# A two-block network on one core: a list scheduler that keeps GpSimd and VectorE apart, with new TensorE durations and a new precedence table

## The chip, the cores and the metric

The kernel runs on one core of a Trainium2 chip (trn2). The core has TensorE (PE, with its weight loads as PEld), VectorE (DVE), ScalarE (ACT), GpSimd (POOL) and SyncE (SP), which issues every DMA here. The metric is the device time of one execution in microseconds (us), lower is better.

## The reference, cut to what matters

Input x is [256, 1024] in float32: 256 tokens. Two blocks follow each other.

```python
# first block
mod = silu(c) @ ada_w + ada_b                  # 6 vectors of 1024: a 1024 x 6144 matrix
u = modulate(rmsnorm(x), sh_mix, sc_mix)
p = u @ w_in                                   # 1024 x 2816
y_conv = conformer_conv(p[..., :1024])         # 31 causal taps on 512 channels, layer norm, silu
y_rwkv = rwkv7_mix(p[..., 1024:])              # 8 heads of 64, a recurrence over the 256 tokens
x = x + gt_mix * (concat(y_conv, y_rwkv) @ w_out)
u = modulate(rmsnorm(x), sh_ffn, sc_ffn)
x = x + gt_ffn * peer_ffn(u)                   # 8 heads, top 16 of 128 x 128 experts; 16384 rows of peer_u, peer_v
x = rmsnorm(x) * final_g
# second block
mod = silu(c_2) @ w_mod_2 + b_mod_2
h = modulate(rms_norm(x)); proj = h @ w_in_2
o_a = dsa_attention(...)                       # keys chosen by an indexer, 4 heads
o_b = moba_attention(...)                      # 4 heads
x = x + gt_m * ((sigmoid(gate_a) * (o_a @ w_br_dsa_2) + sigmoid(gate_b) * (o_b @ w_br_moba_2)) @ w_out_2)
x = x + gt_f * ((silu(g) * u_) @ w_down_2)     # g, u_ = split(modulate(rms_norm(x)) @ w_gate_up_2)
```

## The kernel before

**Arithmetic.** Every float32 weight tile of [128, 1024] is used as a sum of two parts: `wload` (line 1270) issues a DMA of 512 KB into `W_wraw`, a cast into `W_whi`, and a subtraction `W_wlo = W_wraw - W_whi`. Each product is then three products: high by high, high by low, low by high. `W_wraw`, `W_whi` and `W_wlo` have three buffers each, and they are shared by all weight tiles of the program. The experts are not gathered: the hidden values of all 16384 experts are computed (`hidden`, 128 tiles of `peer_u`), multiplied with a grid of gates that is zero but for the chosen experts (`gates`: one-hot tiles `OH_oij` and `OH_oj`, products of them in float16, results into `gH`), and multiplied with all of `peer_v` (`values`, 128 tiles).

**Stages**, in us from the start, where instructions of each first appear on VectorE or PE: modulation and first norm to 58; projections, convolution and RWKV in four chunks (`Mixer`) to 271; output projection, second norm, queries, scores and top 16 of both token tiles (`Peer.scores`, `topk`), with the first hidden columns beside them, to 479; hidden columns and gates to 828; `values` with the second block's modulation beside it to 1175; the final norm to 1196; the second block's projections, attention and second norm to 1455; and the rest of its feed-forward to the end.

**What sets the order.** The program is written as a straight line against recorders. `Recorder.record` (line 81) takes each call down with its dependencies, and `Schedule` (line 282) places them by list scheduling: at each moment each free engine takes the ready instruction with the largest bottom level (the longest chain of costs that hangs on it). [...] `PRIORITY` (line 761) moves the rank of groups of instructions by fixed amounts. Calls through `nc.any` may go to one of two engines: `tensor_tensor`, `tensor_scalar` and `memset` to DVE or POOL, `copy` to ACT or DVE; the engine that is free takes it unless `elsewhere` finds that the other would be done sooner. So `W_wlo`, `OH_oj`, the products into `gH` and others may run on POOL, while calls of `nc.gpsimd` (the convolution's `Afeat_cacc`, products of the modulation matrix in `W_wraw`, `Aprep_yr`, `An_mraw` and `Ach_AB`, `Bt_cand`, `Bt_eq`, `Ca_ropeB`) always do. The finished order is emitted engine by engine through one helper: that is why nearly all instructions carry its line, 663 in the kernel before and 693 in the changed one. On the chip each engine runs its list in that order and waits on semaphores.

Names in rows: `X_u2hi`, `X_u2lo` are the two parts of the normed input of the expert layer, `A_ah`, `A_al` those of the gated hidden values, `Arw_X` and `Arw_XT` the inverses in an RWKV chunk, `Afeat_cacc` the sums of the convolution, `Bt_eq` the comparison of positions in the top 16, `Bt_gate` the gates.

Of the kernel before, what the change touches and what calls it, by code (L numbers as in the profile page):

```python
# [14 lines left out]
P = 128  # L15
# [10 lines left out]
class Op:  # L26
    __slots__ = ("i", "eng", "meth", "args", "kw", "cost", "preds", "succs", "tiles", "regions", "bl", "bias", "tab", "alts",
                 "raw", "half", "cols", "part", "key", "prior")
# [13 lines left out]
class Recorder:  # L42
    """Takes a straight-line program down as a graph of engine instructions, list-schedules it against a cost
    model and emits it in that order through Tile.

    The program is run twice: once on stand-in tiles to find the dependencies, the order and the slot that each
    tile lives in, and once on the real tiles to emit it. Tiles of one tag take their slots in program order."""
# [33 lines left out]
    def record(self, eng, meth, args, kw, alts=()):  # L81
# [10 lines left out]
        op.cols = columns(meth, args) if eng == "PE" else 0.0  # L92
        aps = [a for a in args if isinstance(a, bass.AP)]
# [80 lines left out]
class _Any:  # L174
    """Instructions that the scheduler puts on whichever of several engines is the sooner done with them."""
# [13 lines left out]
    def affine(self, out, a, scale, bias):  # L189
        """out = a * scale + bias, with scale and bias one value per partition."""  # L190
# [14 lines left out]
def cost(op, out, reads):  # L205
    n = _free(out)
    if op.eng == "PE":
# [55 lines left out]
# TensorE's clock: full in a period after one that brought enough columns, else half  # L263
# [11 lines left out]
def latency(a, b):  # L275
    """From the end of a to the start of b, which waits for it."""
# [5 lines left out]
class Schedule:  # L282
    def __init__(self, rec, log=None):
# [20 lines left out]
        # a tile's first op follows the ops of the tile that has its slot before it  # L304
# [12 lines left out]
        # bottom levels; regions count as nodes between the ops they wait for and the ops that use them  # L317
# [21 lines left out]
        # list scheduling  # L339
# [16 lines left out]
        def pick_slot(t):  # L356
            """A slot for tile t, or None: tiles of one tag, and of the tags that share a bank, go in program order."""
# [28 lines left out]
        def elsewhere(op, e):  # L386
            """Whether another engine would be done with op sooner than e, from now."""
# [50 lines left out]
        while done < n:  # L438
            progress = True
            while progress:  # L440
                progress = False
                for e in ENGINES:
                    if busy[e] > now or not avail[e]:
                        continue
                    # best ready op; keep the ones that are not ready aside
                    aside, pick = [], None
                    while avail[e]:
# [4 lines left out]
                        if ready_at[op.i] > now or len(op.alts) > 1 and elsewhere(op, e) or held(op, e):  # L452
# [6 lines left out]
                        if e == "ACT" and op.tab and table[0] not in op.tab and pick is None:  # L459
                            # look for an op near in priority that needs no table load  # L460
# [16 lines left out]
                        if e == "PE" and half[0] and not op.half:  # L477
                            # products of float16 in a row: the weights of a float32 one load beside the product before it
# [240 lines left out]
S = 256  # L719
# [1952 lines left out]
```

## Time and profile before

| what | value |
|---|---|
| time of 3 runs | 1606.6, 1614.03, 1619.74 us; median 1614.03 us |
| span of the profiled execution | 1621.5 us, the only time that the profile gives for it |
| PE busy | 1469.3 us (91%), 9309 matmuls |
| DVE busy | 1353.1 us (83%) |
| ACT busy | 558.4 us (34%) |
| POOL busy | 387.0 us (24%) |
| mean granted TensorE clock | 0.959 of full speed |
| HBM read | 300.23 MB, 187 GB/s over the span |

PE busy counts matmuls whose ends are modelled, and at half the granted clock the same matmul is busy for longer, so 91% is not 91% of what PE could do. DVE busy contains any time in which an instruction has started and is held up, so a change in its mean duration with the same work is a sign of being held up.

### The profile page before, as it was taken

To read this page: it belongs to the slowest core of one execution; us is meant where nothing else is said; L and a number is where in the kernel's file an instruction comes from. 1 tells how busy PE (TensorE), PEld (TensorE's weight loads), DVE (VectorE), ACT (ScalarE), POOL (GpSimd) and SP (SyncE) were. 2 spreads that over 40 slices of the span, in tenths; PEclk is the share of its full clock that TensorE was granted. 3 is DMA by queue.
4 is the path that set the end of the run, shared out by engine and by line. 5 is a ranking of instruction groups with operands and counts; after the bars stand their busy time and mean duration, and the time that the engine had idled before them with its cause. 6 is when DMAs were issued, how large, how long until landed. Compare 5 with 4: busy or idle time off the path is not lost. (4 is left out here: it accounts for less than half of the span.)

```text
span 1621.5 us, 24536 instructions
## 1 busy us (share of the span) xinstructions
PE 1469.3 (91%) x9309; PEld 1308.7 (81%) x9309; DVE 1353.1 (83%) x2241; ACT 558.4 (34%) x1000; POOL 387.0 (24%) x244
## 2 busy tenths in 40 slices
PE   3787788898989999999999999999969999889998
PEld 2676577698989998998988788888846799669987
DVE  6999977798898667888888899989789797887776
ACT  3443434333333222232243333333243365341110
POOL 4577631174462223221200000000043020110000
PEclk9988878999999999999999999999989999999999
DMA  7745433644444533434368988888655543665554
GB/s 275 257 152 158 159 90 130 214 155 157 152 143 143 170 130 131 141 133 138 129 241 252 326 290 293 287 281 300 183 170 183 173 151 123 206 209 184 194 182 143
DMA packets 99222, 305.13 MB, mean 188 GB/s; under 512 B 17952, under 2 KB 24864, under 8 KB 98976
## 3 DMA queue, kind: packets, MB, share of 16 engines
q1 hardware_dynamic: 99104, 303.56, 56.8%
q8 instruction: 73, 1.20, 0.3%
q14 instruction: 45, 0.37, 0.1%
HBM read 300.23 MB, written 3.29 MB: 187 GB/s over the span
## 5 line engine op out<-in xcount | busy, mean ns | idle before, releaser
L663 DVE TENSOR_TENSOR W_wlo<-W_wraw,W_whi 128x1024 fp32r<-128x1024 f32 (+1 forms) x411 | 540.3, 1320 | 28.4 <-ACT W_whi L663 11.5
L663 PE MATMUL bank<-X_u2hi,W_wlo 128*128 128x256 f32 x1088 | 305.0, 290 | 12.5 <-DVE W_wlo L663 11.7
L663 PE MATMUL bank<-X_u2hi,W_whi 128*128 128x256 f32 x1088 | 306.7, 290 | 9.3 <-ACT OH_gel L663 5.3
L663 ACT CAST W_whi<-W_wraw 128x1024 fp32r<-128x1024 f32 (+1 forms) x220 | 229.6, 1046 | 236.0 <-PE bank L663 148.9
L663 PE MATMUL bank<-X_u2lo,W_whi 128*128 128x256 f32 x1088 | 304.1, 288 | 0.0
L663 DVE CAST W_whi<-W_wraw 128x1024 fp32r<-128x1024 f32 (+1 forms) x236 | 170.4, 725 | 114.9 <-PE bank L663 88.7
L663 PEld LDWEIGHTS bank<-X_u2hi,W_wlo 128*128 128x128 f32 x1088 | 208.6, 195 | 15.5 <-DVE W_wlo L663 14.5
L663 PEld LDWEIGHTS bank<-X_u2hi,W_whi 128*128 128x128 f32 x1088 | 209.3, 195 | 11.7 <-ACT OH_gel L663 7.0
L663 PEld LDWEIGHTS bank<-X_u2lo,W_whi 128*128 128x128 f32 x1088 | 209.4, 195 | 0.1
L663 POOL TENSOR_TENSOR W_wlo<-W_wraw,W_whi 128x1024 fp32r<-128x1024 f32 (+2 forms) x45 | 113.3, 2520 | 197.0 <-PE bank L663 102.8
L663 PE MATMUL bank<-W_whi,A_ah 128*128 128x512 f32 x512 | 140.5, 395 | 9.4 <-DVE W_whi L663 4.4
L663 PE MATMUL bank<-W_wlo,A_ah 128*128 128x512 f32 x512 | 140.5, 394 | 1.0 <-DVE W_wlo L663 0.9
L663 PE MATMUL bank<-W_whi,A_al 128*128 128x512 f32 x512 | 139.8, 393 | 0.0
L663 PEld LDWEIGHTS bank<-W_whi,A_ah 128*128 128x128 f32 x512 | 97.3, 191 | 31.3 <-issue 5.5
L663 ACT CAST A_ah<-gH_gH 128x256 fp32r<-128x256 f32 x128 | 51.8, 406 | 185.9 <-PE bank L663 184.9
L663 PEld LDWEIGHTS bank<-W_wlo,A_ah 128*128 128x128 f32 x512 | 97.2, 190 | 22.0 <-DVE W_wlo L663 1.7
L663 PEld LDWEIGHTS bank<-W_whi,A_al 128*128 128x128 f32 x512 | 97.4, 190 | 20.4
L663 PE MATMUL bank<-C_chi,W_wlo 128*128 128x256 f32 (+1 forms) x424 | 111.1, 285 | 0.6 <-DVE W_wlo L663 0.5
L663 PE MATMUL bank<-C_chi,W_whi 128*128 128x256 f32 (+1 forms) x424 | 111.5, 284 | 0.1
L663 PE MATMUL bank<-C_clo,W_whi 128*128 128x256 f32 (+1 forms) x424 | 110.8, 284 | 0.0
L663 POOL TENSOR_TENSOR C_cosg<-C_rope,C_gains 128x128 f32<-128x128 f32 x8 | 4.4, 575 | 371.6 <-DMA C_gains<-in_qkgain_dram 371.6
L663 PEld LDWEIGHTS bank<-C_chi,W_wlo 128*128 128x128 f32 (+1 forms) x424 | 75.6, 188 | 1.8 <-DVE W_wlo L663 0.8
(456 smaller groups left out, 2777.3 us busy)
## 6 DMA issues: line engine op xcount, KB each, us to landing
W_wraw<-in_peer_u_dram SPq DMA_DIRECT2D x128, 512.0 KB, 3.4
W_wraw<-in_peer_v_dram SPq DMA_DIRECT2D x128, 512.0 KB, 4.6
A_mraw<-in_wmodT_dram SPq DMA_DIRECT2D x48, 512.0 KB, 5.1
W_wraw<-in_w_gu_dram SPq DMA_DIRECT2D x36, 512.0 KB, 4.0
W_wraw<-in_w_out_dram SPq DMA_DIRECT2D x26, 512.0 KB, 3.7
W_wraw<-in_w_down_dram SPq DMA_DIRECT2D x22, 512.0 KB, 3.9
An_mraw<-in_adaT_dram SPq DMA_DIRECT2D x16, 512.0 KB, 6.4
W_wraw<-in_w_gate_dram SPq DMA_DIRECT2D x16, 512.0 KB, 3.7
```

Of the source, the lines that this page charges most:

```text
L663: return getattr(eng, "tensor_copy" if meth == "copy" and e != "ACT" else meth)(*args, **kw)
```

## The change

The change has three parts. First, the scheduler knows of a port that DVE and POOL share. `shares_port` says of each DVE instruction whether it uses it (two inputs in SBUF, or one plain copy or scalar operation between SBUF tiles); on POOL everything but `memset` and `iota` does. While a POOL instruction that uses it runs, no DVE instruction that uses it is started. An instruction that may go to either engine isn't put on POOL when DVE has, or will soon have, an instruction ready that uses the port. A POOL instruction that starts while DVE holds the port is charged the rest of DVE's instruction.

Second, some TensorE costs change: 128-row float32 products from 217 to 223 ns (small ones from 109 to 223), products of 256 columns from 109 to 120 ns and of 512 columns from 215 to 227 ns, float16 ones of 128 columns from 55 to 118 ns; the extra 54 ns after float16 goes.

Third, `PRIORITY` has 575 entries in place of 397: 228 are new, 50 are gone, 213 have another value. Comments and docstrings are removed too; the program text of the network is otherwise the same.

```diff
+        op.port = meth not in ("memset", "iota") if eng == "POOL" else shares_port(op) if eng in ("DVE", "ACT") else False
...
             if n <= 16:
-                return 109.0
+                return 223.0
...
-            return max(c, 217.0 if m > 64 else 109.0)
+            return max(c, 223.0 if m > 64 else 109.0)
         if rhs.dtype == F32R:
-            return max(n / 2.4 + 2, 105.0) if n >= 192 else 211.0
-        return max(n / 2.4 + 2, 45.0)
+            return (n + 32) / 2.4 if n >= 192 else 4 * n / 2.4 + 8
+        return max(n / 2.4 + 2, 118.0)
...
+def shares_port(op):
+    if op.meth in ("max", "max_index", "match_replace", "tensor_reduce", "memset", "copy_predicated", "reciprocal"):
+        return False
+    reads = [x for x in list(op.args[1:]) + [v for k, v in op.kw.items() if k not in ("out", "accum_out")] if isinstance(x, bass.AP)]
+    big = [r for r in reads if _free(r) > 1]
+    n = sum(1 for r in big if not _is_psum(r))
+    out = op.kw.get("out", op.args[0])
+    return n >= 2 or n == 1 and len(reads) == 1 and not _is_psum(out) and op.meth in ("copy", "tensor_copy", "tensor_scalar")
...
+        port = {"DVE": 0.0, "POOL": 0.0}
+
+        def port_busy(op, e):
+            if e == "DVE":
+                return op.port and port["POOL"] > now
+            if e != "POOL" or len(op.alts) < 2:
+                return False
+            c = op.alts[e]
+            for b, i in avail["DVE"]:
+                o = ops[i]
+                if i != op.i and start[i] is None and o.port and ready_at[i] <= now + c:
+                    return True
+            return any(start[u] is None and ops[u].port and est[u] < now + c - 200.0 for u in soon["DVE"])
...
-                        if ready_at[op.i] > now or len(op.alts) > 1 and elsewhere(op, e) or held(op, e):
+                        if ready_at[op.i] > now or port_busy(op, e) or len(op.alts) > 1 and elsewhere(op, e) or held(op, e):
...
+                    if e == "POOL" and op.port:
+                        c += max(port["DVE"] - now, 0.0)
+                    if e in port and op.port:
+                        port[e] = now + c
                     if e == "PE":
-                        if half[0] and not op.half:
-                            c += 54.0
...
 PRIORITY = {
-    "add C01 scalar_tensor_tensor nsc": -20000.0,
+    "add C01 tensor_mul gtmp": 500.0,
     "add E00": 28000.0,
-    "add E00 tensor_tensor xres": 7000.0,
+    "add E00 tensor_tensor xres": 6000.0,
...
```

In the built programs POOL goes from 249 instructions to 133 and DVE from 2009 to 2136; ACT has 944 and 929, of which activation table loads are 22 and 18; SP and PE keep their counts. All 43 of POOL's `W_wlo` of 1024 columns go to DVE (404 there before, 447 now), and so do all 19 of its `OH_oj` (45, now 64), all 14 of its products into `gH`, and 20 small ones of the RWKV part. Three places show it.

The top 16 of the experts, on POOL: candidates (`Bt_cand`) and comparisons (`Bt_eq`) of the first token tile. Before:

```order
L663 TENSOR_TENSOR Bt_cand_2225<-Bt_tv_2215 128x256
L663 TENSOR_TENSOR W_wlo_87<-W_wraw_82,W_whi_85 128x1024
L663 TENSOR_TENSOR Bt_cand_2226<-Bt_tv_2215 128x256
L663 TENSOR_TENSOR W_wlo_88<-W_wraw_83,W_whi_84 128x1024
L663 TENSOR_TENSOR W_wlo_89<-W_wraw_81,W_whi_86 128x1024
L663 TENSOR_TENSOR W_wlo_87<-W_wraw_82,W_whi_85 128x1024
L663 TENSOR_TENSOR Bt_eq_2240<-Bt_eq_2240,Bt_ixf_2234 128x2048
L663 TENSOR_TENSOR W_wlo_89<-W_wraw_82,W_whi_86 128x1024
```

and now:

```order
L693 TENSOR_TENSOR Bt_cand_2218<-Bt_tv_2206 128x256
L693 TENSOR_TENSOR Bt_cand_2216<-Bt_tv_2206 128x256
L693 TENSOR_TENSOR Bt_cand_2217<-Bt_tv_2206 128x256
L693 TENSOR_TENSOR Bt_eq_2231<-Bt_eq_2231,Bt_ixf_2225 128x2048
L693 TENSOR_TENSOR Bt_cand_2218<-Bt_tv_2207 128x256
```

The low parts of the weights are gone from POOL, and the candidates and comparisons stand alone.

The same place on DVE, from the sum of the gates to the instructions that follow the second cast. Before:

```order
L663 CAST Bt_ixf_2234<-Bt_tix_2217 128x256
L663 TENSOR_REDUCE Bt_gsum_2232<-Bt_gate_2230 128x8
L663 CAST Bt_abf_2239<-Bt_ab_2237 128x128
L663 RECIPROCAL Bt_gsum_2232<-Bt_gsum_2232 128x8
L663 TENSOR_TENSOR Bt_gate_2230<-Bt_gate_2230,Bt_gsum_2232 128x128
L663 TENSOR_TENSOR Bt_eq_2240<-Bt_abf_2238,Bk_iota_2197 128x2048
L663 TENSOR_TENSOR W_wlo_88<-W_wraw_83,W_whi_84 128x1024
L663 CAST W_whi_85<-W_wraw_81 128x1024
```

and now:

```order
L693 TENSOR_TENSOR Bt_gate_2221<-Bt_gate_2221,Bt_gsum_2223 128x128
L693 TENSOR_TENSOR Bt_eq_2231<-Bt_abf_2229,Bk_iota_2190 128x2048
L693 MAX_INDEX Bt_tix_2208<-Bt_tv_2206,Bt_sc_2204 128x8
L693 MAX_INDEX Bt_tix_2208<-Bt_tv_2206,Bt_s_1_2211 128x8
L693 TENSOR_SCALAR Bt_ab_2228<-Bt_pos_2214 128x128
L693 CAST Bt_ixf_2225<-Bt_tix_2208 128x256
L693 CAST Bt_abf_2230<-Bt_ab_2228 128x128
L693 TENSOR_TENSOR W_wlo_89<-W_wraw_82,W_whi_84 128x1024
L693 MAX Bt_tv_2207<-Bt_sc_2205 128x8 x2
L693 MATCH_REPLACE Bt_s_0_2210<-Bt_tv_2207,Bt_sc_2205 128x128
```

The gates (`Bt_gate`) now stand ahead of `Bt_ixf`, which POOL's comparison waits for, and after one `W_wlo` the searches of the second token tile follow.

The RWKV part on DVE, around the first masked copies into `Arw_X` and `Arw_XT`, which PE waits for. Before:

```order
L663 SCALAR_TENSOR_TENSOR Afeat_cacc_105<-Afeat_convy_104,G_cols_72,Afeat_cacc_105 128x256 x8
L663 TENSOR_TENSOR Aprep_av_120<-bank_60,Afeat_xs_103 128x512
L663 TENSOR_TENSOR Aprep_av_120<-bank_62,Afeat_xs_103 128x512
L663 SCALAR_TENSOR_TENSOR Afeat_cacc_105<-Afeat_convy_104,G_cols_72,Afeat_cacc_105 128x256 x7
L663 COPY_PREDICATED Arw_X_1251<-Afeat_clev_95,bank_64 128x16x16
L663 COPY_PREDICATED Arw_XT_1253<-Afeat_clev_95,bank_63 128x16x16
L663 SCALAR_TENSOR_TENSOR Afeat_cacc_105<-Afeat_convy_104,G_cols_72,Afeat_cacc_105 128x256 x8
```

and now:

```order
L693 TENSOR_TENSOR Ach_W_462<-Ach_W_462,Aprep_fs_124 128x512
L693 TENSOR_TENSOR Ach_W_463<-Ach_W_463,Aprep_fs_124 128x512
L693 SCALAR_TENSOR_TENSOR Afeat_cacc_105<-Afeat_convy_104,G_cols_72,Afeat_cacc_105 128x256 x2
L693 COPY_PREDICATED Arw_X_1251<-Afeat_clev_95,bank_64 128x16x16
L693 COPY_PREDICATED Arw_XT_1253<-Afeat_clev_95,bank_63 128x16x16
L693 SCALAR_TENSOR_TENSOR Afeat_cacc_105<-Afeat_convy_104,G_cols_72,Afeat_cacc_105 128x256 x4
L693 COPY_PREDICATED Arw_XT_1253<-Afeat_clev_95,bank_63 128x8x32
L693 SCALAR_TENSOR_TENSOR Afeat_cacc_105<-Afeat_convy_104,G_cols_72,Afeat_cacc_105 128x256
```

Two sums of the convolution stand ahead of the copies where there were seven in a row, and three products into `Ach_W`, which POOL did, have come in.

## Rows read from the trace of the kernel before

**Rows 1.** The page, busy us, share of the span, instructions.

```profile
PE 1469.3 (91%) x9309; PEld 1308.7 (81%) x9309; DVE 1353.1 (83%) x2241; ACT 558.4 (34%) x1000; POOL 387.0 (24%) x244
```

**Rows 2.** Windows: stretch, length, busy of PE, PEld, DVE, ACT, POOL; clock, DMA, GB/s.

```profile
0.00:58.00 58.00, 27.22 (x151) 23.41 (x152) 42.34 (x83) 18.85 (x35) 24.66 (x24) 0.91 0.78 278
58.00:271.00 213.00, 170.91 (x1155) 150.64 (x1155) 188.40 (x285) 94.01 (x177) 117.68 (x87) 0.85 0.46 147
271.00:479.00 208.00, 184.53 (x1308) 171.44 (x1306) 187.69 (x511) 75.93 (x107) 104.90 (x52) 0.94 0.49 162
479.00:828.00 349.00, 332.48 (x2705) 325.66 (x2705) 279.69 (x382) 102.84 (x219) 82.00 (x41) 0.99 0.43 141
828.00:1175.00 347.00, 344.20 (x1503) 283.77 (x1501) 301.05 (x435) 113.95 (x187) 0.00 (x0) 0.99 0.84 279
1196.00:1455.00 259.00, 237.34 (x1356) 196.94 (x1356) 220.15 (x368) 122.90 (x217) 49.10 (x27) 0.98 0.54 176
```

**Rows 3.** Who PE waited for, 58 to 271 us: total us, times, longest.

```profile
PE bank L663 <- DVE Arw_X L663: 8.0, 3, 7.2
PE bank L663 <- DVE Arw_XT L663: 7.8, 1, 7.8
```

**Rows 4.** Timeline of DVE, 166 to 185 us: start, us, instruction, count.

```profile
165.62 2.85 DVE L663 SCALAR_TENSOR_TENSOR Afeat_cacc<-Afeat_convy,G_cols,Afeat_cacc 128x256 f32<-128x256 f32 x7
...
169.58 10.49 DVE L663 SCALAR_TENSOR_TENSOR Afeat_cacc<-Afeat_convy,G_cols,Afeat_cacc 128x256 f32<-128x256 f32 x7
180.00 0.42 DVE L663 COPY_PREDICATED Arw_X<-Afeat_clev,bank 128x256 f32<-128x256 uint8 x1
```

**Rows 5.** Timeline of POOL, same stretch.

```profile
176.41 2.52 POOL L663 TENSOR_TENSOR W_wraw<-W_wraw,Afeat_cvec 128x1024 f32<-128x1024 f32 x1
```

**Rows 6.** Timeline of DVE, 190 to 212 us.

```profile
193.19 12.24 DVE L663 SCALAR_TENSOR_TENSOR Afeat_cacc<-Afeat_convy,G_cols,Afeat_cacc 128x256 f32<-128x256 f32 x10
```

**Rows 7.** Timeline of POOL, then of DVE, 457 to 468 us.

```profile
460.65 5.52 POOL L663 TENSOR_TENSOR Bt_eq<-Bt_eq,Bt_ixf 128x2048 f32<-128x2048 f32 x1 [0.37 <-DVE Bt_ixf L663]
...
461.69 4.62 DVE L663 TENSOR_TENSOR Bt_gate<-Bt_gate,Bt_gsum 128x128 f32<-128x128 f32 x1
```

**Rows 8.** Who PE waited for, 457 to 468 us; then the window behind it.

```profile
PE bank L663 <- DVE W_whi L663: 3.7, 1, 3.7
...
465.80:472.60 6.80, 5.63 (x26) 5.63 (x27) 6.66 (x6) 0.00 (x0) 2.74 (x2) 0.50 0.27 86
```

**Rows 9.** DVE groups by form, 900 to 1150 us, with POOL idle: busy us, mean ns.

```profile
L663 DVE TENSOR_TENSOR W_wlo<-W_wraw,W_whi 128x1024 fp32r<-128x1024 f32 x93 | 113.8, 1224 | 4.8 <-ACT W_whi L663 2.9
```

**Rows 10.** Groups by form, 271 to 479 us: DVE, then POOL.

```profile
L663 DVE TENSOR_TENSOR W_wlo<-W_wraw,W_whi 128x1024 fp32r<-128x1024 f32 x37 | 58.3, 1583 | 3.7 <-ACT W_whi L663 2.2 <-PE bank L663 0.6
...
L663 POOL TENSOR_TENSOR W_wlo<-W_wraw,W_whi 128x1024 fp32r<-128x1024 f32 x25 | 62.5, 2505 | 47.4 <-PE bank L663 30.3 <-DVE W_whi L663 8.5 <-ACT W_whi L663 7.7
```

**Rows 11.** DVE groups by form, 479 to 828 us.

```profile
L663 DVE TENSOR_TENSOR W_wlo<-W_wraw,W_whi 128x1024 fp32r<-128x1024 f32 x86 | 124.0, 1452 | 6.5 <-ACT W_whi L663 3.0 <-PE bank L663 2.5
L663 DVE TENSOR_TENSOR OH_oij<-Bk_iota,Bk_ijT 128x1024 f16<-128x1024 f16 x62 | 51.1, 844 | 10.5 <-PE bank L663 10.4
```

**Rows 12.** Tiles `OH_oj` and `W_wlo`, 479 to 828 us: min, median, max ns.

```profile
L663 DVE TENSOR_TENSOR OH_oj<-OH_oij,Bk_gT x44: 677/681/2890, 486.9 to 816.2; 128x1024 f16<-128x1024 f16 x44
...
L663 POOL TENSOR_TENSOR W_wlo<-W_wraw,W_whi x9: 2366/2393/3263, 487.7 to 807.7; 128x1024 fp32r<-128x1024 f32 x9
```

**Rows 13.** Who PE waited for, 271 to 479 us.

```profile
PE bank L663 <- DVE W_wlo L663: 7.9, 8, 2.6
```

**Rows 14.** Who PE waited for, 479 to 828 us.

```profile
PE bank L663 <- DVE W_wlo L663: 6.1, 8, 1.0
```

**Rows 15.** The chain that ended last, in order of time: start, us, what.

```profile
1408.24 2.21 POOL G_xres L663
```

**Rows 16.** Timeline of DVE, 1404 to 1420 us.

```profile
1410.30 0.70 DVE L663 TENSOR_TENSOR G_xres<-G_xres,C_gtmp 128x512 f32<-128x512 f32 x1
```

**Rows 17.** POOL groups by form, 58 to 271 us.

```profile
L663 POOL TENSOR_TENSOR W_wlo<-W_wraw,W_whi 128x1024 fp32r<-128x1024 f32 x6 | 15.4, 2576 | 4.7 <-PE bank L663 4.6
```

More of the change, by code (lines that the diff above doesn't have):

```diff
@@ L27 @@
     __slots__ = ("i", "eng", "meth", "args", "kw", "cost", "preds", "succs", "tiles", "regions", "bl", "bias", "tab", "alts",
-                 "raw", "half", "cols", "part", "key", "prior")
+                 "raw", "half", "cols", "part", "key", "prior", "port")
 def _free(ap):
@@ new lines @@
+    "hidden4": 8000.0,
+    "hidden4 activation gH1": -2000.0,
+    "hidden4 activation gel": 20000.0,
+    "hidden4 copy whi": 16000.0,
+    "hidden4 dma_start wraw": 18000.0,
+    "hidden4 matmul h": -30000.0,
+    "hidden4 tensor_tensor gH1": 500.0,
+    "hidden5": -4000.0,
+    "hidden5 activation gH1": 7000.0,
+    "hidden5 activation gel": 6500.0,
+    "hidden5 tensor_tensor gH1": 16000.0,
+    "hidden6": -1000.0,
+    "hidden6 activation gH1": -5000.0,
+    "hidden6 activation gel": 500.0,
@@ L922 @@
-    "merge tensor_sub clo": -2000.0,
-    "mods activation AB": -1000.0,
-    "mods dma_start yr": -1000.0,
-    "mods scalar_tensor_tensor AB": -1000.0,
-    "norm h0": -2000.0,
-    "norm h0 copy chi": 1000.0,
-    "norm h0 transpose n": -48000.0,
+    "merge tensor_add mg": -1000.0,
+    "merge tensor_sub clo": -3000.0,
+    "mods activation AB": -5000.0,
+    "mods dma_start yr": -2000.0,
+    "mods late activation wraw": -2000.0,
+    "mods scalar_tensor_tensor AB": -1000.0,
+    "mods tensor_tensor AB": -32000.0,
@@ L970 @@
     "norm u20": -4000.0,
[L971 to L974 removed]
+    "norm u20 activation nrs": 1000.0,
+    "norm u20 activation sqjunk": 5000.0,
+    "norm u20 copy u2hi": 8000.0,
     "norm u20 reciprocal nrr": 4000.0,
[L976 to L979 removed]
@@ L1093 @@
+    "side dma_start gtf": -6000.0,
+    "side scalar_tensor_tensor mraw": 29000.0,
+    "side tensor_add mod": -3000.0,
+    "side tensor_scalar rowcol": -4000.0,
+    "split00": 16000.0,
+    "split00 copy mixhi": -33000.0,
+    "split00 tensor_sub mixlo": -2000.0,
+    "split40": -58000.0,
+    "split40 copy mixhi": -38000.0,
+    "split40 tensor_sub mixlo": 46000.0,
+    "split4128": -4000.0,
+    "split4128 tensor_sub mixlo": 2000.0,
     "state0": -8000.0,
-    "state0 copy R": 1000.0,
     "state0 copy VS": 8000.0,
-    "state0 matmul m": 4000.0,
+    "state0 copy yr": 4000.0,
@@ new lines @@
+    "state2 matmul m": 3000.0,
+    "state2 tensor_add VS": -53000.0,
+    "state2 tensor_add yr": -8000.0,
+    "state2 tensor_copy VS": -10000.0,
+    "state3 copy R": -55000.0,
+    "state3 copy VS": -12500.0,
+    "state3 copy yr": 500.0,
+    "state3 tensor_copy VS": -2500.0,
+    "sums0": -4000.0,
+    "sums0 copy gH1": -17000.0,
+    "sums0 matmul g": 2500.0,
+    "sums0 tensor_mul gH0": 4500.0,
+    "sums0 tensor_tensor oij": 1000.0,
+    "sums1": -2000.0,
+    "sums1 copy gH0": 56000.0,
@@ L1120 @@
+    "sums1 copy gH1": -500.0,
+    "sums1 matmul g": 32000.0,
+    "sums1 tensor_mul gH1": 4000.0,
+    "sums1 tensor_tensor oj": -42000.0,
+    "sums2 copy gH1": -32000.0,
+    "sums2 tensor_mul gH0": -27500.0,
+    "sums2 tensor_tensor oij": 30000.0,
+    "sums3 copy gH1": -8000.0,
+    "sums3 matmul g": 3000.0,
+    "sums3 tensor_tensor oj": 25000.0,
+    "tail": 63000.0,
+    "tail dma_start dram": 2000.0,
+    "tail tensor_mul outt": -9000.0,
+    "tail tensor_tensor outt": -1000.0,
     "topk0": 4000.0,
-    "topk0 activation gate": 4000.0,
@@ new lines @@
+    "values0 dma_start wraw": 32000.0,
+    "values0 matmul o": 4000.0,
+    "values0 tensor_sub al": -2000.0,
+    "values0 tensor_tensor wlo": -1000.0,
+    "values1 copy ah": -1000.0,
+    "values1 copy whi": 1500.0,
+    "values1 matmul o": 4000.0,
+    "values1 tensor_sub al": -34000.0,
+    "values1 tensor_tensor wlo": 2000.0,
+    "values2": 2000.0,
+    "values2 copy whi": -32000.0,
+    "values2 tensor_sub al": 32000.0,
+    "values3": 9500.0,
+    "values3 dma_start wraw": -80000.0,
+    "values3 matmul o": -9000.0,
```

612 lines of the change are left out of this document (360 added, 252 removed).

## The prediction

> **What bounds the kernel now.** I read the page first, then the windows by stage, then the waits of PE and the timelines around its longest ones. PE is busy for 1469.3 of 1621.5 us and DVE for 1353.1 [rows 1], so no engine is a bound on its own over the whole span; the windows say where each is [rows 2]. From 828 to 1175 us PE is busy for 344.2 of 347 at a clock of 0.99: nothing is to be had there. From 479 to 828 it is busy for 332.5 of 349 (16.5 idle). The losses lie earlier and later: 213 - 170.9 = 42.1 us idle from 58 to 271, and there the clock is 0.85, which makes the busy time itself too long; 208 - 184.5 = 23.5 idle from 271 to 479 at 0.94; 259 - 237.3 = 21.7 idle from 1196 to 1455. In the two early stages DVE is busy for 188.4 of 213 and 187.7 of 208. So they are bound by DVE's queue and by chains that pass through it, and PE idles when something it needs stands too far back in that queue.
>
> What makes the queue slow can be read from durations. With POOL idle a `W_wlo` takes DVE 1224 ns [rows 9]; from 271 to 479 the mean is 1583 [rows 10], from 479 to 828 it is 1452 [rows 11], with the same shape. The timelines show why. Seven sums of the convolution take 2.85 us together at 165.62, and the next seven take 10.49 [rows 4], while POOL multiplies modulation tiles of 2.52 us each [rows 5]; behind them stands the copy into `Arw_X`, and PE's longest wait for it is 7.2 us [rows 3]. Ten more take 12.24 us [rows 6] where 10 x 2.85 / 7 = 4.1 would do, and PE waits 7.8 us for `Arw_XT` [rows 3]. At 461.69 a product of 128 columns takes 4.62 us, until the `Bt_eq` of POOL that began at 460.65 is over [rows 7]; the cast behind it is late and PE stands for 3.7 us, and in the next 6.8 us its granted clock is 0.50, the lower of its two levels (1.2 GHz), with 5.63 us of matmuls [rows 8]: another 2.8 us lost, since half of these would do at 2.4 GHz. So a stall of this size costs itself and 2.8 more.
>
> **The change, part by part.**
>
> *Work that moves from POOL to DVE, 271 to 479 us.* 25 `W_wlo` took POOL 2505 ns each [rows 10] and go to DVE at 1224 [rows 9]: +30.6 us on DVE. Given back: the 37 that were there shrink from 1583 to 1224, -13.3 us. Net +17 on DVE, which has 208 - 187.7 = 20.3 us idle [rows 2]. It fits by 3 us; I cost it at 0, and if DVE's idle time can't be used, at up to +17.
>
> *The same, 479 to 828 us.* 9 `W_wlo` [rows 12] at 1.224 are +11.0, and the 19 `OH_oj` at their median of 681 ns on DVE [rows 12] +12.9 (one of them lies earlier). Given back: 86 x (1452 - 1224) ns = 19.6, and 62 `OH_oij` from 844 [rows 11] to the 681 of the equally large `OH_oj`, 10.1. Net -6 on DVE, where 69 us are idle. Cost 0. The products into `gH` are 14 in the whole program and of at most 512 columns: at about half of a `W_wlo`, 0.6 us, at most +8 on DVE, covered by the same idle time.
>
> *The same, 58 to 271 us.* 6 `W_wlo` [rows 17] at 1.224 are +7.3. The 20 small RWKV ones have no more than 512 columns: at most 0.6 us each, +12, and the four fills of 1024 columns at most 1.2 each, +5. Together +24 at most, against the two runs of sums that were held up by 10.49 - 2.85 = 7.6 and 12.24 - 4.1 = 8.1, -15.7 if all of it went. POOL keeps the sums and the modulation products, so it won't all go. Net between +24 and +8, with 213 - 188.4 = 24.6 us idle as cover.
>
> *Stalls in the RWKV stage.* The two waits of 7.2 and 7.8 us are there because seven and ten sums stood ahead of a copy that PE needs, and POOL came between them. Now two stand ahead of the first copies, and one to four between later ones, and DVE's masked copy reads PSUM and doesn't count as a user of the port. What speaks against a full gain is the order's own accuracy: it was made with costs, and POOL's products start when a DMA lands. I take half of the two waits, -7.5, and half of the two times 2.8 us at the low clock behind them, -2.8: **-10**. Bounds: -20.6 (all) and 0.
>
> *The stall at the gates.* `Bt_gate` now precedes the cast that POOL's `Bt_eq` waits for, so it can't be held up by it; after one `W_wlo` the searches follow, which don't use the port. 3.7 + 2.8: **-6.5**, bounds -6.5 and 0 (a `W_wlo` that starts just after POOL did would wait instead).
>
> *Waits for `W_wlo`.* PE waits 7.9 us for DVE's from 271 to 479 [rows 13] and 6.1 from 479 to 828 [rows 14], 16 times about 0.9 us, roughly what a `W_wlo` on POOL or one held up is late. Some remain as plain lateness in a full queue. I take **-8** of the 14; bounds -14 and +17 (above).
>
> *The second block.* In the chain that ended last, one sum into `xres` takes POOL 2.21 us [rows 15]; its neighbour takes DVE 0.70 [rows 16]. All three of POOL's go to DVE, and so do the products of the final norm: **-3** (1.5 at this chain, the same again at the final norm). Bounds -6 and 0.
>
> *TensorE's costs, the table, the loads.* New costs change no instruction, only ranks; SP issues as many DMAs as before, and at the start two modulation tiles now precede the first weight tile. All of it is in the order and has no row of its own. I cost it at 0: what it moves off one chain it can put on another. Bounds: half of the idle time that my terms don't touch. That is 42.1 + 23.5 + 16.5 + 21.7 = 103.8, less the 15 + 3.7 + 14 + 1.5 named, about 70; so -35, and the same to the other side is held to +10, as the table's entries keep their form.
>
> Sum: -10 - 6.5 - 8 - 3 = -27.5, say **-28** against the span of 1621.5, so 1593. That execution lies above all three runs shown; the median of them is 1614, and 1614 - 28 = **1586 us**.
>
> **The rivals.**
>
> *DVE becomes the bound (slower).* It takes work of 127 more instructions, and where it is nearly full that is lengthening: +17 from 271 to 479, up to +24 less the idle time it can't use from 58 to 271, say +10, with no stall gained. 1614 + 27 = 1641. For it: DVE is busy for 88 and 90% in these stages. Against it: the idle times of 20 and 25 us, and that POOL's work was holding DVE up by almost as much as it carried. It decides where the moved work goes beyond what is given back plus the idle time. The Trainium skill, "Perfetto Trace Analysis", Optimizing Scalar/DVE Operations, says that with VectorE saturated it may make sense to offload some work, even to GpSimd; this change does the reverse. The same passage adds that, as the two share a port, moving work between them may not help; the stretched `W_wlo` above agree with that second half. By the first half alone the time would be that 1641. Chance 0.13.
>
> *The port is freed but the gaps move (no change).* The waits that go are replaced by others of the same chains: RWKV's recurrence is serial, and DVE's load there hardly falls. Only the second block's -3 and some of the small waits remain, -3 to -10: 1604 to 1611. A form of it is that the change doesn't do what it says: POOL and DVE drift from the planned times, POOL's own sums and products still meet DVE's, and each meeting costs as before. For it: all of `Afeat_cacc` and the modulation products stay on POOL. Chance 0.27.
>
> *The table closes much more.* The orders of all stages are new, and about 70 us of idle time stand outside my terms. With half of them and all of the stalls: 1614 - 35 - 28 = 1551. Chance 0.14.
>
> **How the numbers follow.** My forecast has 0.46. About 1% (16 us) is what a measurement of this kernel can tell from no change, so faster means below 1598 and slower above 1630. Faster: 0.46 and 0.14, of which I leave out 0.01 for the edge: 0.59. Same: 0.27. Slower: 0.13, and 0.01 for the edge: 0.14. The range holds the forecast's own bounds on most terms (1614 - 20.6 - 6.5 - 14 - 6 = 1567 with all named stalls gone, 1614 with none), the no-change case and the large gain but for its tail, and leaves out most of the slower rival: 1550 to 1626.
>
> **What would show each step.** Right: `W_wlo` on DVE near 1230 ns in all stages; no `W_wlo` or `OH_oj` on POOL; POOL busy near half of 387 us; runs of convolution sums near 0.41 us each; no wait of PE above 5 us between 58 and 271 and a clock above 0.85 there; no wait of several us at the gates. Wrong: DVE busy above 195 of the 208 us of that stage (271 to 479) with PE's waits for `W_wlo` or `W_whi` longer than before; runs of sums as stretched as before; or the same idle time of PE in a stage under other names. What would upset the forecast most is a first gate product so much later that hidden columns run out before the gates are done.

## The result, and the profile after

The changed kernel takes 1573.26 us (median of 4 runs, 1568.62 to 1574.32) against 1614.53 us: a ratio of 0.9738, 95% interval 0.9704 to 0.9771. The forecast was 1586, 13 us more: a gain of 28 us was forecast and one of 41 measured. The number held; most places where the forecast looked for the gain did not.

The page after; its second line answers to [rows 1], the third is the group of DVE's `W_wlo` (busy us, mean ns, idle before):

```profile
span 1566.9 us, 24537 instructions
...
PE 1438.9 (92%) x9309; PEld 1285.0 (82%) x9309; DVE 1332.5 (85%) x2368; ACT 539.0 (34%) x985; POOL 161.3 (10%) x128
...
L693 DVE TENSOR_TENSOR W_wlo<-W_wraw,W_whi 128x1024 fp32r<-128x1024 f32 (+1 forms) x456 | 559.4, 1233 | 51.2 <-ACT W_whi L693 32.5
```

POOL fell from 387 us to 161, and DVE, which took the work over, is busy for 20 us less: its `W_wlo` take 1233 ns in the mean of the whole program, where they took 1320. By stage, those of 1024 columns take 1312 ns from 253 to 461 us and 1266 from 461 to 787, where they took 1583 and 1452 [rows 10, 11]; that is nearer to the 1224 of [rows 9], but not all the way. PE's own busy time fell by 30 us with the same matmuls, while its mean granted clock rose from 0.959 to 0.975. The stages, in the columns of [rows 2]:

```profile
57.00:253.00 196.00, 159.06 (x1160) 141.87 (x1159) 168.47 (x323) 98.70 (x181) 72.40 (x59) 0.89 0.47 154
253.00:461.00 208.00, 181.06 (x1303) 167.69 (x1301) 195.37 (x538) 69.39 (x98) 40.11 (x23) 0.95 0.48 162
461.00:787.00 326.00, 324.54 (x2708) 322.11 (x2708) 275.21 (x437) 83.32 (x207) 0.00 (x0) 1.00 0.44 152
```

From 461 to 787 PE idles for 1.5 us where it idled for 16.5. From 253 to 461 DVE is busy for 195.4 of 208, and PE idles for 26.9, more than the 23.5 of [rows 2]. Two long waits of PE, one in each of the early stages, are new in this size (the one for `Bt_gate` was 3.1 us before; total us, times, longest; the last line answers to [rows 13]):

```profile
PE bank L693 <- DVE Arw_VS L693: 13.2, 3, 12.5
...
PE bank L693 <- DVE Bt_gate L693: 13.5, 1, 13.5
PE bank L693 <- DVE W_wlo L693: 6.1, 9, 1.9
```

DVE's timeline at the first: 30 sums of the convolution stand ahead of the sum into `Arw_VS`, a tile of the recurrence. They take 0.40 us each, so nothing holds them up; they are simply ahead.

```profile
201.56 11.95 DVE L693 SCALAR_TENSOR_TENSOR Afeat_cacc<-Afeat_convy,G_cols,Afeat_cacc 128x256 f32<-128x256 f32 x30
213.54 0.43 DVE L693 TENSOR_TENSOR Arw_VS<-bank,Arw_S0f 64x256 f32<-64x256 f32 x1
```

The windows of the second wait and of the time behind it:

```profile
328.00:341.00 13.00, 0.00 (x0) 0.00 (x0) 13.00 (x76) 1.50 (x2) 1.24 (x2) 0.65 0.00 1
341.50:359.00 17.50, 15.74 (x103) 15.14 (x104) 17.10 (x61) 4.48 (x6) 7.76 (x3) 0.78 0.35 112
```

For 13 us PE does nothing, DVE is busy for 13.00 us, POOL for 1.24, and the granted clock stays below full behind it.

**A ledger of PE's losses.** Stages of two orders can't be compared by the clock alone, since each does other work in them. So for each matmul I took the time from its start to the next one's start, less the 30th percentile of that time over the matmuls with the same operands in all 14 traces. What is left is loss: idle time, low clock, slow pitch. The pitches sum to 1356.0 to 1356.1 us in every kernel, so the sums of the losses compare. The cuts are at the last product of the first projections, the last of the recurrence, the first one of the one-hot tiles, the last hidden column, the last value product:

| us lost | start | recurrence | to first gate product | gates and hidden | values | second block | sum |
|---|---|---|---|---|---|---|---|
| before | 67.0 | 53.9 | 32.8 | 31.0 | 18.1 | 56.6 | 259.4 |
| after | 57.3 | 31.7 | 54.1 | 1.6 | 13.1 | 46.7 | 204.5 |
| difference | -9.7 | -22.2 | +21.3 | -29.4 | -5.0 | -9.9 | -54.9 |

The sum is the difference of the two spans (54.6), and that is 13 us more than the 41.3 by which the medians differ: each ledger is of one profiled execution, the one of the kernel before was longer than all its four timed runs, and the one of the changed kernel was its fastest. In which columns these 13 us lie isn't known. Below, those of e1 and e10 ran 5.6 and 4.6 us faster than their medians, those of e4, e5 and e7 4.6, 4.4 and 10.4 slower.

The columns don't compare as well as the sums, since their borders are PE's and the other engines' work moves across them. In the kernel before, the first gate product stands ahead of the top 16 of the second token tile, and 35 us of DVE's top-16 instructions lie behind it; in the changed one 3 us do. So a part of what leaves the column of the gates is only in the column ahead of it now. Two other stretches are free of this. From the last product of the first projections to the last hidden column (three columns together, "middle" below) the loss fell from 117.7 to 87.4 us, by 30.3. From DVE's last instruction of the top 16 to the last hidden column ("late gates") it fell from 21.9 to 0.7.

### The profile page after: what moved, and what is told of

Same layout as the page of the kernel before. It is cut to its first block, busy times and chain, and to the rows that moved or that the text cites. A ratio compares the mean times of both kernels' runs of the same rounds, so it can differ in the third digit from the quotient of the medians.

```text
span 1566.9 us, 24537 instructions
## 1 busy us (share of the span) xinstructions
PE 1438.9 (92%) x9309; PEld 1285.0 (82%) x9309; DVE 1332.5 (85%) x2368; ACT 539.0 (34%) x985; POOL 161.3 (10%) x128
## 3 DMA queue, kind: packets, MB, share of 16 engines
q1 hardware_dynamic: 99104, 303.56, 57.3%
## 4 chain that ended last, share of the span: by engine, by line
PE 64%; DVE 21%; DMA 8%; issue 3%; ACT 3%; SPq 0%; DVEq 0%; ACTq 0%
PE bank L693 64%; DVE W_wlo L693 6%; DMA W_wraw<-in_peer_v_dram 2%; DVE W_whi L693 2%; DVE Afeat_cacc L693 1%; ACT W_whi L693 1%; DMA W_wraw<-in_w_out_dram 1%; DMA W_wraw<-in_peer_wqa_dram 1%; DVE Ach_ZR L693 1%; DVE Bt_tix L693 1%; DMA W_wraw<-in_w_qka_dram 1%; DMA row<-A_rowcol 1%; DVE Bt_pos L693 1%; DVE An_mraw L693 1%; DVE Bt_tv L693 1%
## 5 line engine op out<-in xcount | busy, mean ns | idle before, releaser
L693 DVE TENSOR_TENSOR W_wlo<-W_wraw,W_whi 128x1024 fp32r<-128x1024 f32 (+1 forms) x456 | 559.4, 1233 | 51.2 <-ACT W_whi L693 32.5
L693 ACT CAST W_whi<-W_wraw 128x1024 fp32r<-128x1024 f32 (+1 forms) x212 | 221.4, 1046 | 241.3 <-PE bank L693 157.6
L693 PE MATMUL bank<-X_u2hi,W_wlo 128*128 128x256 f32 x1088 | 296.4, 286 | 4.8 <-DVE W_wlo L693 4.7
L693 PE MATMUL bank<-X_u2hi,W_whi 128*128 128x256 f32 x1088 | 297.1, 285 | 0.2 <-ACT W_whi L693 0.2
L693 PE MATMUL bank<-X_u2lo,W_whi 128*128 128x256 f32 x1088 | 295.4, 284 | 0.0
L693 PEld LDWEIGHTS bank<-X_u2hi,W_wlo 128*128 128x128 f32 x1088 | 202.4, 192 | 6.4 <-DVE W_wlo L693 6.2
L693 PEld LDWEIGHTS bank<-X_u2hi,W_whi 128*128 128x128 f32 x1088 | 203.1, 192 | 0.5 <-ACT W_whi L693 0.4
L693 PEld LDWEIGHTS bank<-X_u2lo,W_whi 128*128 128x128 f32 x1088 | 202.8, 192 | 0.1
L693 PEld LDWEIGHTS bank<-W_wlo,A_ah 128*128 128x128 f32 x512 | 96.5, 189 | 21.8 <-DVE W_wlo L693 1.7
L693 PEld LDWEIGHTS bank<-W_whi,A_al 128*128 128x128 f32 x512 | 96.0, 188 | 21.6 <-DVE A_al L693 1.4
L693 PE MATMUL bank<-C_chi,W_whi 128*128 128x256 f32 (+1 forms) x424 | 105.4, 284 | 1.3 <-ACT Ca_sg L693 1.0
L693 PEld LDWEIGHTS bank<-C_chi,W_whi 128*128 128x128 f32 (+1 forms) x424 | 73.2, 187 | 2.7 <-ACT Ca_sg L693 1.4
```

What stands on the lines that cost most here:

```text
L693: return getattr(eng, "tensor_copy" if meth == "copy" and e != "ACT" else meth)(*args, **kw)
```

## The experiments

Theory P says that the freed port carries the gain, theory O that the order does. The change has three parts (rules of the port, TensorE's costs, table), so kernels with each alone and each pair can be made, and besides these the placement can be changed within one order. "Stretch" is DVE's time beyond the median of equally shaped instructions that met none of POOL's (counting every overlap makes the numbers up to 15 us larger, with the same grouping); "gates" is that column of the ledger, "late gates" and "middle" are the two stretches named behind it.

| kernel | rules, costs, table | ratio to before, 95% | stretch us | gates us | late gates us | middle us | all losses us |
|---|---|---|---|---|---|---|---|
| before | - - - | 1 | 131 | 31.0 | 21.9 | 117.7 | 259.4 |
| after | x x x | 0.9738, 0.9704 to 0.9771 | 31 | 1.6 | 0.7 | 87.4 | 204.5 |
| e1 | placement alone | 1.0042, 1.0020 to 1.0064 | 61 | 23.4 | 7.3 | 111.5 | 254.5 |
| e2 | order alone | 1.0050, 1.0033 to 1.0068 | 114 | 22.4 | 18.2 | 126.1 | 263.0 |
| e3 | - x x | 1.0120, 1.0084 to 1.0156 | 110 | 31.0 | 13.9 | 129.2 | 274.2 |
| e4 | x x - | 1.0028, 1.0008 to 1.0047 | 30 | 7.3 | 7.2 | 114.2 | 263.6 |
| e5 | x - x | 0.9851, 0.9817 to 0.9886 | 35 | 5.8 | 2.2 | 97.1 | 233.6 |
| e6 | x - - | 1.0111, 1.0074 to 1.0148 | 33 | 9.0 | 5.0 | 121.6 | 269.8 |
| e7 | - x - | 1.0315, 1.0278 to 1.0352 | 149 | 75.6 | 59.8 | 167.2 | 315.8 |
| e9 | - - x | 1.0060, 1.0036 to 1.0084 | 137 | 35.3 | 21.8 | 122.7 | 262.8 |

**e1: the kernel before, POOL's optional work issued on DVE.**

```diff
             e = rec.ops[i].eng
+            if e == "POOL" and rec.ops[i].alts:
+                e = "DVE"
```

> The kernel before, in its own order on every engine; only the 121 instructions that its scheduler had put on POOL by choice (45 W_wlo, 19 OH_oj, 14 products into gH, RWKV's small ones) are issued on DVE, each at its planned place. POOL keeps its own sums and products. Theory P (the port: what POOL did by choice stretched DVE's instructions, by about 80 us summed over the trace of before): the median W_wlo of DVE falls from 1320 to about 1235 ns and the time to 1575 to 1595 us, without any new order. Theory O (the order: the gain comes of ranks made with right durations): DVE gets the 127 instructions, its mean W_wlo falls too, but PE's waits stay where the order puts them: 1605 to 1640 us.

1624.77 us, within O's range and far from P's. `W_wlo` of DVE fell to a mean of 1248 ns and a median of 1221, as P said (1320 is the mean before, not the median), and POOL to 154.3 us; DVE took the work and rose only from 1353.1 to 1360.6 us. So the moved work is indeed paid for by what DVE gets back. PE loses 14.6 us less in the late gates, and the program is no shorter for it. The convolution's sums keep their stretch, since POOL's own products still meet them (DVE groups from 58 to 253 us: before, then e1, then after):

```profile
L663 DVE SCALAR_TENSOR_TENSOR Afeat_cacc<-Afeat_convy,G_cols,Afeat_cacc 128x256 f32<-128x256 f32 x60 | 43.4, 787 | 0.1
```

```profile
L665 DVE SCALAR_TENSOR_TENSOR Afeat_cacc<-Afeat_convy,G_cols,Afeat_cacc 128x256 f32<-128x256 f32 x60 | 43.1, 782 | 0.1
```

```profile
L693 DVE SCALAR_TENSOR_TENSOR Afeat_cacc<-Afeat_convy,G_cols,Afeat_cacc 128x256 f32<-128x256 f32 x60 | 27.3, 524 | 0.1
```

**e2: the changed kernel's order, the same work back on POOL.**

```diff
+ON_POOL = {121, 130, 181, ...}
...
             e = rec.ops[i].eng
+            if i in ON_POOL:
+                e = "POOL"
```

> The changed kernel, in its own order; only the 117 instructions that POOL did before and DVE does now go back to POOL, each at its place in the new order. Theory P: the stretching comes back, W_wlo on DVE at 1300 ns or more, and with it most of the gain is lost: 1600 to 1620 us. Theory O: the new order carries the gain, and DVE is relieved a little as well: 1560 to 1585 us.

1626.62 us: the whole gain is gone, more than P said (its mean `W_wlo`, 1286 ns, is under P's 1300). PE waits 10.2 us for POOL's `W_wlo` (min, median, max ns), which are late for an order that counts on DVE's 1.2 us, and 8.3 for `Cn_xn`, the second block's normed input, on POOL; the rest is spread over many waits:

```profile
L696 POOL TENSOR_TENSOR W_wlo<-W_wraw,W_whi x45: 1411/2402/9030, 31.8 to 1394.4; 128x1024 fp32r<-128x1024 f32 x43, 128x768 fp32r<-128x768 f32 x1, 128x576 fp32r<-128x576 f32 x1
```

So neither half carries the gain alone. In the late gates, though, the placement does: 21.9 us against 7.3 in the order before, 18.2 against 0.7 in the new one.

**e3: without the rules (first diff); e4: with the table of before (second).**

```diff
-                        if ready_at[op.i] > now or port_busy(op, e) or len(op.alts) > 1 and elsewhere(op, e) or held(op, e):
+                        if ready_at[op.i] > now or len(op.alts) > 1 and elsewhere(op, e) or held(op, e):
...
-                    if e == "POOL" and op.port:
-                        c += max(port["DVE"] - now, 0.0)
```

```diff
 PRIORITY = {
-    "add C01 tensor_mul gtmp": 500.0,
+    "add C01 scalar_tensor_tensor nsc": -20000.0,
...
```

> The changed kernel without the port rules: TensorE's new costs and the new precedence table stay, the scheduler may put 101 instructions on POOL by choice (30 W_wlo among them). Theory P: 1600 to 1620 us, and DVE's W_wlo above 1300 ns. Theory O: 1570 to 1590 us. The table was made with the rules on, so a part of a loss may be the misfit of the two; POOL's share and the stretched durations tell that apart.

> The changed kernel with the precedence table of before: port rules and TensorE's new costs stay. Theory P: the port rules do the work, 1575 to 1595 us. Theory O in the form that the table does it: 1600 to 1630 us; the stalls of PE would then be at other places than in the changed kernel, with DVE's W_wlo still near 1235 ns.

1638.32 us, outside both ranges, and 1623.37, in O's. Both lose all of the gain; e3's mean `W_wlo` is 1272 ns, not 1300. e3's table was made with the rules on, so a misfit of the two is in its loss as well as the port. In e4 the stretch is as small as after and the gates lose 7.3 us, yet all other stages lose more: the middle 26.8 us more than in the changed kernel, the first stage 73.3 against 57.3. PE's waits in the first stage, of e4 and of the changed kernel, up to 60 us (`An_nu` is the first norm's result; the text on e10 says `An_xn`):

```profile
PE bank L693 <- ACT An_nu L691: 33.1, 1, 33.1
```

```profile
PE bank L693 <- ACT An_nu L691: 12.6, 1, 12.6
```

**e5: with TensorE's old costs.** **e6: the rules alone,** the kernel before with the lines that e3 takes out. **e7: the new costs alone,** the kernel before with this diff of e5 the other way round.

```diff
-                return 223.0
+                return 109.0
...
-        return max(n / 2.4 + 2, 118.0)
+        return max(n / 2.4 + 2, 45.0)
...
+                        if half[0] and not op.half:
+                            c += 54.0
```

> The changed kernel with TensorE's costs of before: port rules and new table stay. If TensorE's durations only shift ranks (theory A), a per cent at most is lost: 1573 to 1590 us, and PE's loss from the first gate product to the last hidden column stays near the 1.6 us of the changed kernel. If an order that is right for DVE needs PE's true pace as well (theory B), this stage loses 15 us or more again and the time is 1600 to 1640 us.

> The kernel before with the port rules alone: old costs, old table. The same scheduler choice that took POOL's optional work off in the changed kernel, without what came with it. Theory A: 1590 to 1605 us, most of the loss from the first gate product to the last hidden column (30.9 us before) gone. Theory B: 1610 to 1640 us, this stage still losing 15 us or more, as it did when the same work was only issued on DVE (23.4 us).

> The kernel before with TensorE's new costs alone: POOL keeps its optional work (32 W_wlo by the new order), old table. Theory A: no gain, 1605 to 1630 us, the gates stage loses 25 to 31 us as before, since DVE is still stretched by POOL. Theory B (costs matter by themselves): that stage loses 10 to 20 us, and the time is 1590 to 1610 us if nothing else gets worse.

1593.37, 1634.65 and 1669.59 us: e5 and e7 lie outside both theories, e6 has B's time. The costs are worth about 1% beside the other two parts (e5 against after) and lose 3% alone. In e7's gates PE waits (446 to 876 us) for DVE, most of all for `W_wlo`; that POOL's stretch is all of it isn't shown, as e9 has nearly the same stretch and less than half of the loss:

```profile
PE bank L691 <- DVE W_wlo L691: 26.8, 16, 2.3
```

The gates column splits cleanly: 1.6 to 9.0 us in the four kernels with the rules, 31.0 to 75.6 in the four without. But so does the place of the second top 16: 1 to 3 us of it lie behind the first gate product in those with the rules, 33 to 54 in those without. The late gates are free of that and split by the placement: 0.7 to 7.3 us in the five kernels whose optional work is off POOL but for a few instructions, e1 among them, 13.9 to 59.8 in the five where it is on POOL. So on this stage A was right for e6, by 17 us. Its time is B's because it loses 26 us more than the kernel before between the first projections and the first gate product, and 5 more at the start (30.8 us for `An_nu`). Over the middle, the rules alone (e6) and the rules with the costs (e4) give next to nothing; with the table they give 20.6 (e5), and with all three 30.3.

**e8: POOL may take `W_wlo` of the first hidden columns.**

```diff
-            if e != "POOL" or len(op.alts) < 2:
+            if e != "POOL" or len(op.alts) < 2 or op.key in FREE:
                 return False
...
+FREE = {"hidden0 tensor_tensor wlo"}
```

> The changed kernel, but the rule that keeps optional work off POOL isn't asked for the W_wlo of the first group of hidden columns: 7 of them go to POOL while DVE searches the top 16 (12 optional instructions on POOL, 5 in the changed kernel). Theory C (the new wait of 13.5 us for Bt_gate is there because only DVE may make W_wlo, and it is full of searches, which don't use the port): the wait shrinks below 5 us, most of the half clock behind it goes, 1550 to 1565 us. Rival D (the chain of the top 16 itself sets the end of this stage, or POOL's W_wlo stretch DVE's again): 1570 to 1585 us, with the idle time under another name.

1568.32 us, ratio 0.9701 (0.9670 to 0.9733), between C and D; its interval overlaps that of the changed kernel. C's mechanism is shown: windows from 320 us, of the changed kernel and of e8.

```profile
320.00:340.00 20.00, 7.28 (x57) 6.68 (x56) 20.00 (x106) 5.87 (x8) 3.32 (x4) 0.80 0.15 53
```

```profile
320.00:340.00 20.00, 20.00 (x168) 19.89 (x167) 20.00 (x104) 10.91 (x12) 16.69 (x10) 1.00 0.50 173
340.00:360.00 20.00, 15.48 (x113) 14.71 (x112) 12.75 (x37) 8.20 (x11) 7.83 (x4) 0.91 0.26 91
...
400.00:420.00 20.00, 17.23 (x137) 16.36 (x136) 19.46 (x60) 9.19 (x12) 1.25 (x2) 1.00 0.40 134
```

PE goes from 7.28 to 20.00 of 20 us, and the wait for `Bt_gate` from 13.5 to 2.2. The hole was there because the rule left `W_wlo` to DVE alone while DVE searched the top 16, and POOL stood idle. The other kernels bear this out: PE waits for `Bt_gate` for 12.0 to 13.9 us at a time in all with the rules and no exception (the changed one, e4, e5, e6, e10, e11) and in e2, which has their order, and for 1.9 to 6.4 in all without (before, e1, e3, e7, e9), whatever the table. So this wait is the price of the rule and not of the new ranks. But 7 `W_wlo` later some of the time is lost again (15.48 and 17.23 of 20 us): the ledger's third column falls only from 54.1 to 47.9. And 4.4 of these 6 us go again in the second block (46.7 to 51.1), where the order is another one too; both are of single executions.

The Trainium skill ("Perfetto Trace Analysis", Optimizing Scalar/DVE Operations) says that work of a saturated VectorE may be worth giving even to GpSimd, and that the shared port may spoil it. Here the trace agrees with both halves: with the first in these 20 us, with the second where e2 takes all of it back.

**e9: the table alone,** the kernel before with e4's diff the other way round. **e10: e4 with the new table's entries for the start** (85 in place of 63).

```diff
+START = ("consts", "mods", "norm u0", "norm u2", "norm u4", "norm u6", "proj")
 PRIORITY = {
-    entries of the old table whose group is in START
+    entries of the new table whose group is in START
```

> The kernel before with the new precedence table alone: no port rules, old TensorE costs, 118 optional instructions on POOL. Theory E (the three parts need each other: ranks that fit need the rules and the right pace): no gain, 1610 to 1640 us, with DVE's W_wlo above 1280 ns and a loss of PE of 25 us or more from the first gate product to the last hidden column, as in every kernel without the rules so far. Rival F (the table is what brings the gain, and the rules only spoil the other combinations): 1580 to 1600 us.

> The kernel of e4 (port rules, new costs, old table), but the groups of the start (constants, modulation, first norm, first projections: 100 entries or so) have the new table's values. e4 had one wait of 33.1 us for An_xn at 14 to 47 us, where the changed kernel has 12.6; PE's loss to the last of the first projections was 73.3 us there, 57.3 in the changed kernel. Theory G (the table pays stage by stage, each stage by itself): that wait is below 15 us and about 16 us come back, 1600 to 1612 us. Rival H (the orders hang together, what is won at the start is lost behind it): 1615 to 1630 us.

e9 took 1627.22 us: E, not F, with a mean `W_wlo` of 1273 ns (E said above 1280). e10 took 1614.93 us, ratio 0.9980 (0.9958 to 1.0002), between G and H. Its wait is 12.6 us again, as G said, the same as the changed kernel's above. The start's loss fell from 73.3 to 63.1 us, 10 of the 16 that G said, and the time by 8.4 (by 7.8 if the two sessions' ratios are taken). So the table pays in part stage by stage: mending one wait gives back 10 of the 16 us that e4 lacks at the start, and the rest of its lack lies in all later stages.

**e11: `Arw_VS` ahead of the 30 sums; e12: e8 with a table fitted to it.**

```diff
-    "state2 tensor_add VS": -53000.0,
+    "state2 tensor_add VS": 20000.0,
```

```diff
-    "sums2 tensor_mul gH0": -27500.0,
+    "sums2 tensor_mul gH0": -57000.0,
...
-    "topk1 tensor_tensor cand": 8000.0,
+    "topk1 tensor_tensor cand": 9000.0,
```

> The changed kernel with one entry of the table changed: the sum into Arw_VS of the third chunk goes from -53000 to +20000, so that it no longer stands behind 30 sums of the convolution (11.95 us) on DVE. Theory I (the new wait of 12.5 us for Arw_VS is a free mistake of the order): the wait goes, and with it some of the half clock behind it: 1555 to 1565 us. Rival K (the 30 sums have to be done by DVE in this stretch anyway, and PE then waits for the convolution or the output projection): the wait goes, another of 5 to 15 us takes its place, 1570 to 1590 us.

> The kernel of e8 (POOL may take W_wlo of the first hidden columns) with 12 entries of the table changed for it. e8 closed the wait for Bt_gate (13.5 us to 2.2) and gave most of it back in small waits behind it. Theory L (these are small misfits of the table to the new places, as in the other combinations): another 3 to 8 us, 1558 to 1566 us. Rival M (what is left is DVE's load in these stages): 1566 to 1572 us.

e11 took 1578.69 us, ratio 0.9758 (0.9731 to 0.9785), not to be told apart from the changed kernel, and in K's range: the wait of 12.5 us went, and two others came (190 to 260 us):

```profile
PE bank L693 <- DVE Afeat_cacc L693: 13.4, 1, 13.4
PE bank L693 <- ACT Amix_mixhi L693: 6.0, 1, 6.0
```

The recurrence's loss fell by 12.1 us and the next stage's rose by 20.9. So moving this sum alone wins nothing, as K said: the 30 sums are due by then. That no other order could hide them isn't shown; e12 keeps the wait of 12.5 us.

e12 took 1564.47 us, ratio 0.9672 (0.9646 to 0.9698), L's range and the best of all: 9 us under the changed kernel by the medians and 11 by the ratios, which are from different sessions and whose intervals just don't meet. 451 entries of the table differ from e8's, not 12 (the diff shows two). So it shows that a new fit of the whole table wins again, and can't tell L's small misfits from anything else that the table sets.

## Why the prediction was right, and where it was not

**Moved work at 0: right for the sum of DVE's time.** DVE took over nearly all of POOL's optional work and is busy for less; e1 shows the balance without a new order, +7.5 us of DVE's time in the whole span.

**Stalls in the RWKV stage, -10: the named waits went, the sum did not.** PE's waits for `Arw_X` and `Arw_XT` [rows 3] are gone and the recurrence lost 22.2 us less. But with the stage behind it, up to the first gate product, the balance is -0.9: the 13.5 us for `Bt_gate` are in it, and the wait for `Arw_VS`, which e11 could only move. Of the signs that I gave, the clock came (0.89); the others failed: two waits above 5 us are there (12.5 and, for `Afeat_xs`, 5.9), and the sums are at 0.52 us, not 0.41. A sign of being wrong that I gave came true in the next stage: the same idle time of PE under other names, 26.9 us for 23.5.

**The stall at the gates, -6.5: right where it stood, and replaced.** `Bt_eq` no longer holds up a gate product that PE waits for [rows 7, 8]. The 13.5 us for `Bt_gate` came in an earlier place. The step that failed: I moved `W_wlo` off POOL at a cost of DVE's time alone, with 20 us of idle time as cover. I didn't ask when in the stage that idle time lies. While DVE searches there is none, and no other engine could make `W_wlo`. The prediction's upset case named a first gate product so late that hidden columns run out; it was these columns' weights that ran out. That e4 and e6 have this wait with the old table shows that it comes with the rules.

**Waits for `W_wlo`, -8: right in size.** They went from 7.9 [rows 13] to 6.1 us and from 6.1 [rows 14] to 0.5: -7.4.

**Second block, -3:** -9.9, mis-sized; I priced three sums of `xres` and had no term for the order.

**TensorE's costs and the table at 0: this step failed most.** Start, values and the second block beyond its -3 lost 21.6 us less (9.7, 5.0 and 6.9), for which I had no term; the middle lost 30.3 less, where my terms for it sum to 24.5. The 13 us that the ledger has over the medians are somewhere in these numbers. Without the table the whole gain is gone (e4), without the costs some two fifths of it (e5), and the table alone gives none (e9). The late gates are the exception: there the placement gives most (7.3 us left in e1 and 5.0 in e6, of 21.9), and waits for `OH_gel` (5.3 us) and `gH` (0.8), of which I had no term, went too. With the old table the kernels with the rules lose as much again ahead of the gates.

**The rivals.** That the port is freed and the gaps move (1604 to 1611) is what e1, e4 and e6 show when a part is missing: stretch down by 70 to 100 us, time the same or worse. DVE as the bound did come true, for 13 us at one place. That the table closes much more was the right direction: 41 us, where the forecast had 28 and this rival 63. The total of the forecast came as near as 13 us by luck: waits that I counted as gone came back under other names, and parts that I had put at 0 gave a gain.

What stays open: which single entries of the table do the work behind the start, and why e10 gave back 10 us there and not 16. A rival is untested: no table was fitted anew for the scheduler without the rules or with the old costs. The new table has 575 entries for 397, and e12 wins by fitting once more. So how much of the gain needs the rules, and how much is only a longer fit of the table, isn't shown; shown is that this table needs the rules (e3, e9) and that the rules need a table made for them (e4, e6).

## What to carry to other kernels

Freeing an engine from contention shortened its instructions here, and the program only where nothing else was in the way: the gain came when the order was planned with the contention in it, and a table of ranks must be fitted again after a change of the rules. A rule that keeps work off an engine needs an exception where the engine that must do it instead is full, so look at the idle time of a stage piece by piece and not as a sum. Compare two orders by losses at equal work, and set the borders of stages where no engine's work can move across them: a border at one engine's landmark showed a gain of 29.4 us at the gates, of which 21.2 are left once the border stands behind the top 16.

## What the runs showed of the hardware

A DVE instruction with two inputs in SBUF that starts while a product runs on POOL mostly ends after POOL's, however small it is: of 212 `W_wlo` of 1024 columns that started so in the 14 traces, 202 did, with a median of 1.08 us behind POOL's end. The others went through, and so did 37 of 182 sums of the convolution; the longest such case is in e2, where sums ran beside a `W_wlo` of POOL that took 9.03 us. In e8 the normalisation of the gates, 0.27 us in the changed kernel, took 2.21, until the `W_wlo` on POOL ended (timelines of DVE, then POOL), and PE's remaining wait of 2.2 us is this:

```profile
342.64 2.21 DVE L694 TENSOR_TENSOR Bt_gate<-Bt_gate,Bt_gsum 128x128 f32<-128x128 f32 x1
...
342.35 2.35 POOL L694 TENSOR_TENSOR W_wlo<-W_wraw,W_whi 128x1024 fp32r<-128x1024 f32 x1 [1.51 <-ACT W_whi L694]
```

The Trainium skill ("SBUF — State Buffer", Who interferes with whom) says that a VectorE instruction with two inputs in SBUF contends with a GpSimd instruction that reads SBUF, over a pair of ports that is an exclusive lock; this trace agrees.

The rules don't count DVE's operation with one input tile and a scalar per partition as a user of the port. The changed kernel shows that this one is (0.41 us alone):

```profile
145.78 2.39 DVE L693 TENSOR_SCALAR Afeat_cacc<-Afeat_convy,G_cols 128x256 f32<-128x256 f32 x1
...
145.67 2.36 POOL L693 TENSOR_TENSOR W_wraw<-W_wraw,Afeat_cvec 128x1024 f32<-128x1024 f32 x1
```

It ends 0.15 us after POOL's product. That `tensor_scalar` can take the shared pair is in the Trainium skill too ("SBUF — State Buffer", Who interferes with whom), and the trace agrees. Searches are not held up: in the kernel before, 43 index searches of 128 columns under POOL's instructions have a median of 281 ns, 9 alone 282.
